# The last product of a decoder block by one level of Strassen, with sums and LayerNorm in PSUM

## The chip, the cores and the metric

The kernel runs on one core of a Trainium2 chip. A core has five engines with a queue of instructions each: TensorE (PE), VectorE (DVE), ScalarE (ACT), GpSimd (POOL) and SyncE (SP), which here only issues DMAs. They meet through semaphores. Matmuls write to PSUM, which PE, DVE and ACT use here; everything else lies in SBUF (128 partitions) or in DRAM. The metric is the device time of one execution in microseconds; "us" below always means that.

## The reference

One block of a decoder: x is 2048 x 1024 in float32. A projection feeds two branches, a dilated attention and a gated linear recurrence; each is projected to 1024 columns and the two are merged by gates. Only the end concerns this change:

```
merged = sigmoid(gA) * yA + sigmoid(gB) * yB
out    = merged @ W_out + b_out          # (2048 x 1024) @ (1024 x 1024)
x      = LayerNorm(alpha * x + out)      # alpha = 2 ** 0.25, eps = 1e-5, gain and bias by column
```

Here yA = o @ w_attn_proj, with 512 columns of attention output o. `y_a` in the text is this product, `z` is merged @ W_out.

## The kernel before

Products in float32 are made of pieces: each operand is split into a high part h (a rounded copy by ACT) and a low part l (the rest, one subtraction on DVE), and a product is h·h + h·l + l·h, three matmuls for each 128 of the inner dimension. A matmul has a stationary tile of 128 x 128 and moves 512 columns as a rule.

The program has four stages. **Stage A** is the input projection, 507 products of 12 matmuls (line 634), already by one level of Strassen; beside it a planner starts chains of work (ropes, gates, the recurrence, blocks of weights). A chain is a generator that yields an `Ask`: it goes on once a given number of products has passed, enough buffers are vacant, and each engine it names still has budget at this product (`left`). The helper `tt` (line 227) records most of DVE's operations, so they show up under its line. **Attention** comes second (lines 1038 to 1103), the 32 jobs of y_b third (lines 1370 to 1376). The **last stage** has:

- `ya_job(i)` (lines 1440 to 1454), 32 jobs (four chunks of 512 rows, eight blocks of 128 columns): 12 matmuls; DVE multiplies by the gate, reading PSUM (line 1453); POOL adds y_b and writes the merged piece `me` (line 1454). The loads of the gate `gA` and of `ybr` stand on SP.
- `out_job(tt)` (lines 1469 to 1525), 16 row tiles of 128 rows: 48 matmuls into two PSUM banks (lines 1480 to 1482), with `mh`, `ml` of the tile as stationary side and W_out as moving one. `split_m` makes them for the next tile (ACT line 1466, DVE line 1467). Then DVE makes alpha·x + b_out (line 1489), adds both banks (1493), takes statistics (1496, 1499); ACT the root (1513); DVE three small refinements (1515 to 1519), and centre, gain and bias (1503, 1523); ACT's queue issues the stores.
- The first 8 `ya_job`s run alone; the other 24 stand between the row tiles, two to four after a tile, so that their loads and their DVE and POOL work spread over z.
- W_out is split by `split` (lines 1132, 1133) piece by piece, in the eight first `ya_job`s and before.

The order in this stage is that of the code: it is written out by hand, and each engine runs its own queue in it. `later(n, fn)` puts work off by n jobs; `big(slot, ...)` gives one of the large SBUF buffers, X0 to X5 and Z0 to Z2, whose earlier tenant must be done.

Of the kernel before, what the change touches and what calls it, by code (L numbers as in the profile page):

```python
# [31 lines left out]
def hybrid_block_kernel(ctx: ExitStack, tc: tile.TileContext, a: dict, out: bass.AP):  # L32
# [1319 lines left out]
    cmb = {4 + (3 * i) // 2: divmod(i, 4) for i in range(16)}
    wo = [(k, j) for k in range(4) for j in range(2)] + [(4, 0), (5, 0), (4, 1), (5, 1), (6, 0), (7, 0), (6, 1), (7, 1)]
# [37 lines left out]
    for n in range(32):  # L1391
        c, f = divmod(n, 8)
        if c + 1 < NCH:
            for k in range(2 * f, 2 * f + 2) if f < 4 else ():
                load_h(c + 1, k, min(k + 2, 7) - f)
        elif f < 4:
            for k in range(2 * f, 2 * f + 2):
                prep_wa(k, k + 2 - f if k < 6 else 4)
        if n in (12, 14, 28, 29, 30, 31):
            load_wo({12: 0, 14: 1, 28: 2, 29: 3, 30: 4, 31: 5}[n])  # L1400
# [37 lines left out]
    ME, XR, MS = {}, {}, {}  # L1438

    def ya_job(i):  # L1440
        c, f = divmod(i, 8)
        if i + 3 < 8 or 11 <= i + 3 < 32:
            load_ya(i + 3)
        ga, yb = YG.pop(i)
        ya = fp.tile([P, CH], F32, tag="y", name=f"ya{c}{f}", bufs=4)
# [5 lines left out]
        if f == 0:  # L1451
            ME[c] = big(("Z0", "Z1")[c % 2], [P, 8, CH], F32, f"me{c}")
        dve.scalar_tensor_tensor(out=ga, in0=ga, scalar=1.0, in1=ya, op0=ALU.add, op1=ALU.mult)
        pool.tensor_tensor(out=ME[c][:, f], in0=ga, in1=yb, op=ALU.add)
# [5 lines left out]
    def split_m(tt, ks=slice(0, 8)):  # L1460
        c, b = divmod(tt, 4)
        m = ME[c][:, ks, b * P:(b + 1) * P]
        if ks.start == 0:
            MS[tt] = tuple(vx_p.tile([P, 8, P], F32R, tag=t, name=f"{t}{tt}", bufs=2) for t in ("mh", "ml"))
        mh, ml = (t[:, ks] for t in MS[tt])
        act.activation(mh, m, AF.Copy)
        dve.tensor_tensor(out=ml, in0=m, in1=flat(mh), op=ALU.subtract)

    def out_job(tt):
        rows = slice(tt * P, (tt + 1) * P)  # L1470
        x = XR.pop(tt)
        mh, ml = MS.pop(tt)
        last = tt == 15
        parts = [slice(0, CH), slice(CH, CH + 256), slice(CH + 256, D)] if last else [slice(0, CH), slice(CH, D)]
        zz = [fp.tile([P, CH], F32, tag="z", name=f"z{tt}{n}", bufs=3)[:, 0:hs.stop - hs.start] for n, hs in enumerate(parts)]
        for k0, k1 in ((0, 6), (6, 8)) if tt == 0 else ((0, 8),) if tt % 4 else ((0, 7), (7, 8)):
            for z, hs in zip(zz, parts):
                for k in range(k0, k1):
                    w = WO[k]
                    pe.matmul(z, mh[:, k], w[:, 0, hs], start=(k == 0), stop=False)  # L1480
                    pe.matmul(z, mh[:, k], w[:, 1, hs], start=False, stop=False)  # L1481
                    pe.matmul(z, ml[:, k], w[:, 0, hs], start=False, stop=(k == 7))  # L1482
        if tt + 1 < 16:
            load_xr(tt + 1)
            split_m(tt + 1, slice(0, 8 if (tt + 1) % 4 else 7))
        if tt == 1:
            for fn in at1:
                fn()
        dve.scalar_tensor_tensor(out=x, in0=x, scalar=ALPHA, in1=vec[0], op0=ALU.mult, op1=ALU.add)
        st_ = cst.tile([P, 4, 6], F32, tag="st", name=f"st{tt}", bufs=2)  # L1490
        n = 0
        for z, hs in zip(zz, parts):
            dve.tensor_tensor(out=x[:, hs], in0=x[:, hs], in1=z, op=ALU.add)
            step = 256 if last else CH
            for q in range(hs.start, hs.stop, step):
                dve.bn_stats(out=st_[:, n, :], in_=x[:, q:q + step])
                n += 1
        mv = cst.tile([P, 4], F32, tag="mv", name=f"mv{tt}", bufs=2)
        dve.bn_aggr(out=mv[:, 0:2], in_=st_[:, 0:n])
        halves = (slice(0, CH), slice(CH, D))  # L1500

        def centre(hs):
            dve.scalar_tensor_tensor(out=x[:, hs], in0=x[:, hs], scalar=mv[:, 0:1], in1=vec[1][:, hs],
                                     op0=ALU.subtract, op1=ALU.mult)

        if last:
            pool.memset(mv[:, 3:4], -0.5)
            pool.tensor_tensor(out=mv[:, 2:3], in0=mv[:, 1:2], in1=epst, op=ALU.add)
            pool.tensor_tensor(out=mv[:, 2:3], in0=mv[:, 2:3], in1=mv[:, 3:4], op=ALU.pow)
            for hs in halves:  # L1510
                centre(hs)
        else:
            act.activation(mv[:, 2:3], mv[:, 1:2], AF.Sqrt, bias=epst)
            centre(halves[0])
            dve.reciprocal(out=mv[:, 2:3], in_=mv[:, 2:3])

            dve.tensor_scalar(out=mv[:, 1:2], in0=mv[:, 1:2], scalar1=EPS, scalar2=-0.5, op0=ALU.add, op1=ALU.mult)
            dve.scalar_tensor_tensor(out=mv[:, 3:4], in0=mv[:, 2:3], scalar=mv[:, 2:3], in1=mv[:, 1:2], op0=ALU.mult, op1=ALU.mult)
            dve.tensor_scalar(out=mv[:, 2:3], in0=mv[:, 3:4], scalar1=1.5, scalar2=mv[:, 2:3], op0=ALU.add, op1=ALU.mult)
        for hs, eng in zip(halves, (sp, act) if last else (act, act)):  # L1520
            if hs.start and not last:
                centre(hs)
            dve.scalar_tensor_tensor(out=x[:, hs], in0=x[:, hs], scalar=mv[:, 2:3], in1=vec[2][:, hs],
                                     op0=ALU.mult, op1=ALU.add)
            eng.dma_start(out[rows, hs], x[:, hs])
# [12 lines left out]

    def bring_at(c):
        if c < NCH:  # L1540
            for k in range(4):
                load_at(c, k, 1)

    load_xr(0)
    load_vec(0)
    bring_at(1)
    load_vec(1)
    load_vec(2)
    for i in range(8, 11):
        load_ya(i)  # L1550
    now["n"] += 1
    for tt in range(16):
        c, b = divmod(tt, 4)
        run(late)
        out_job(tt)
        if c + 1 < NCH:
            for f in (((0, 1), (2, 3), (4, 5, 6), (7,)) if c else ((), (0, 1, 2), (3, 4, 5, 6), (7,)))[b]:
# [64 lines left out]
```

## Time and profile before

| what | value |
|---|---|
| median of three runs | 2084.6 us (2084.38 to 2085.69) |
| the profiled execution: its time | 2088.65 us |
| its span, first to last instruction | 2086.9 us |
| granted clock of PE, mean | 0.998 |
| first matmul of y_a | 1817.98 us |
| first matmul of z | 1839.74 us |

The profiled execution is the one that all durations come from. In the profile a group is a line, an engine, an operation, out<-in and its shape, with count, busy time and mean in ns; a row of the timeline has its start and its duration, and in brackets the idle time of the engine before it and what ended that. A window row has, for each engine, the busy time and the number of instructions (x), then PE's granted clock, the share of the DMA engines and GB/s. In the chain of waits PE's rows show the time to the next matmul, not the length of one.

### The profile page before, as it was taken

The numbers are of one execution on the slowest core, as the hardware profiler recorded it, in microseconds if no ns is written. First come the engines' busy times: TensorE is split into PE (matmuls) and PEld (weight loads), VectorE is DVE, ScalarE is ACT, GpSimd is POOL, SyncE is SP. The second block draws the span as 40 slices with busy tenths as digits, with TensorE's granted clock in tenths as the row PEclk, the third lists the DMA queues.
The fourth block names the chain that finished last, engine by engine and source line by source line (L and its number), as shares of the span: only waits on it lengthen the run. The fifth ranks groups of instructions, "written<-read, shape, count | busy, mean of one in ns | idle before, by whom it ended". The sixth has DMA issues, their size and how long they took to land.

```text
span 2086.9 us, 35149 instructions
## 1 busy us (share of the span) xinstructions
PE 2066.7 (99%) x11696; PEld 1704.5 (82%) x11696; DVE 1657.9 (79%) x3146; ACT 1101.7 (53%) x2293; POOL 471.6 (23%) x436
## 2 busy tenths in 40 slices
PE   8999999999999999999999999999999999999998
PEld 7888887887878888888887888888888888888887
DVE  8888889788888878778878888877999545576667
ACT  6447356346356565667666657567999411211100
POOL 1111111111111012222222232221425244331120
PEclk9999999999999999999999999999999999999999
DMA  9997988988988977778788979789896898964432
GB/s 277 276 255 240 265 256 240 289 253 264 249 282 236 323 251 195 233 209 242 235 258 261 287 233 266 246 227 365 323 334 196 246 300 276 300 226 159 145 106 71
DMA packets 370358, 516.27 MB, mean 247 GB/s; under 512 B 173824, under 2 KB 178944, under 8 KB 366848
## 3 DMA queue, kind: packets, MB, share of 16 engines
q1 hardware_dynamic: 350000, 480.63, 72.5%
q0 software_dynamic: 12256, 19.42, 5.5%
q10 hardware_dynamic: 7920, 13.97, 1.8%
q8 instruction: 93, 1.52, 0.3%
q14 instruction: 89, 0.73, 0.1%
HBM read 312.95 MB, written 186.25 MB: 239 GB/s over the span
## 4 chain that ended last, share of the span: by engine, by line
PE 66%; ACT 5%; DVE 1%; DMA 0%; issue 0%; DVEq 0%; ACTq 0%
PE q L634 39%; ACT p L1053 4%; PE yb L1370 3%; PE yb L1371 3%; PE z L1480 3%; PE z L1482 3%; PE yb L1372 3%; PE z L1481 3%; PE o L1094 2%; PE s L1038 2%; PE ya L1448 1%; PE ya L1450 1%; PE ya L1449 1%; PE pt L1064 1%; PE g L495 1%; PE bc L1312 1%
## 5 line engine op out<-in xcount | busy, mean ns | idle before, releaser
L634 PE MATMUL q<-xT,hS 128*128 128x512 f32 x1680 | 519.0, 390 | 0.2 <-DVE v L227 0.2
L634 PE MATMUL q<-xT,l 128*128 128x512 f32 x1120 | 435.8, 389 | 0.0
L634 PE MATMUL q<-xB,hA 128*128 128x512 f32 x1248 | 388.6, 393 | 5.6 <-ACT xB L215 5.5
L634 PEld LDWEIGHTS q<-xT,hS 128*128 128x128 f32 x1680 | 314.2, 188 | 70.4 <-issue 5.8
L634 PE MATMUL q<-xB,l 128*128 128x512 f32 x904 | 353.1, 391 | 1.1 <-DVE l L227 1.1
L634 PEld LDWEIGHTS q<-xB,hA 128*128 128x128 f32 x1248 | 235.2, 189 | 58.5 <-ACT xB L215 5.5
L634 PEld LDWEIGHTS q<-xT,l 128*128 128x128 f32 x1120 | 210.2, 188 | 44.0 <-DVE l L227 0.2
L634 PEld LDWEIGHTS q<-xB,l 128*128 128x128 f32 x904 | 170.5, 189 | 37.4 <-DVE l L227 1.9
L1053 ACT ACTIVATE p<-p,sta 128x256 f32<-128x256 f32 (+1 forms) x384 | 172.7, 469 | 1.1 <-DVE sta L1045 1.1
L634 PE MATMUL q<-xT,hA 128*128 128x512 f32 x560 | 173.0, 390 | 0.0
L634 PE MATMUL q<-xB,hS 128*128 128x512 f32 x560 | 172.9, 390 | 0.0
L245 POOL DMA_DIRECT2D wS<-in_w_in_dram x70 | 61.8, 967 | 485.6 <-DMA wS<-in_w_in_dram 174.6
L269 ACT ACTIVATE hA<-wA 128x512 fp32r<-128x512 f32 x218 | 134.2, 623 | 49.8 <-DMA wA<-in_w_in_dram 13.3
L269 ACT ACTIVATE hS<-S 128x512 fp32r<-128x512 f32 x175 | 107.8, 623 | 82.9 <-DVE S L227 17.6
L227 POOL TENSOR_TENSOR S<-S,wA 128x512 f32<-128x512 f32 x35 | 50.0, 1428 | 351.7 <-DVE S L227 266.8
L634 PEld LDWEIGHTS q<-xT,hA 128*128 128x128 f32 x560 | 104.7, 188 | 23.4 <-issue 1.8
L634 PEld LDWEIGHTS q<-xB,hS 128*128 128x128 f32 x560 | 104.8, 188 | 23.1 <-issue 1.5
L1045 DVE CUSTOM_DVE_ANT_0 p<-s,mask 128x256 f32<-128x256 f32 (+1 forms) x384 | 116.5, 360 | 0.2 <-PE s L1038 0.2
L1481 PE MATMUL z<-wo,mh 128*128 128x512 f32 (+1 forms) x264 | 101.0, 383 | 0.0
L1482 PE MATMUL z<-wo,ml 128*128 128x512 f32 (+1 forms) x264 | 101.0, 383 | 0.0
L1480 PE MATMUL z<-wo,mh 128*128 128x512 f32 (+1 forms) x264 | 101.0, 383 | 0.0
L1370 PE MATMUL yb<-h,wl 128*128 128x512 f32 x256 | 100.3, 392 | 0.0
(204 smaller groups left out, 4134.9 us busy)
## 6 DMA issues: line engine op xcount, KB each, us to landing
wA<-in_w_in_dram SPq DMA_DIRECT2D x253, 256.0 KB, 4.7
wl_scr<-l SPq DMA_DIRECT2D x105, 512.0 KB, 5.0
l<-wl_scr SPq DMA_DIRECT2D x105, 512.0 KB, 4.4
sw<-y SPq DMA_DIRECT2D x384, 64.0 KB, 3.2
wS<-in_w_in_dram SPq DMA_DIRECT2D x70, 256.0 KB, 4.6
wS<-in_w_in_dram POOLq DMA_DIRECT2D x70, 256.0 KB, 6.7
v_scr<-vs SPq DMA_DIRECT2D x192, 64.0 KB, 3.6
B<-k_scr SPq DMA_DIRECT2D x24, 512.0 KB, 7.6
```

Of the source, the lines that this page charges most:

```text
L227: eng.tensor_tensor(out=out, in0=in0, in1=in1, op=op)
L245: pool.dma_start(t, w_part(s, x), accum_op=ALU.add)
L269: act.activation(h, r, AF.Copy)
L634: pe.matmul(bank, w[:, ks], x[:, kk, xx], start=(first and i == 0 and not onto), stop=(last and i == 11), skip_group_check=onto)
L1045: dve.tensor_tensor_reduce(out=st["p", i, j][:, h, lo:256], in0=st["s", i, j // 2][h][:, j % 2, lo:256], in1=mask[:, lo:256], scale=1.0, s ...
L1053: act.activation(p, p, AF.Exp, scale=-1.0, bias=s[:, h:h + 1], accum_out=s[:, 2 + h:3 + h])
L1370: pe.matmul(yb, WL[f][:, 0, k], xx[:, 0], start=(k == 0), stop=False)
L1371: pe.matmul(yb, WL[f][:, 0, k], xx[:, 1], start=False, stop=False)
L1372: pe.matmul(yb, WL[f][:, 1, k], xx[:, 0], start=False, stop=(k == 7))
L1480: pe.matmul(z, mh[:, k], w[:, 0, hs], start=(k == 0), stop=False)
L1481: pe.matmul(z, mh[:, k], w[:, 1, hs], start=False, stop=False)
L1482: pe.matmul(z, ml[:, k], w[:, 0, hs], start=False, stop=(k == 7))
```

## The change

1. **Blocks of W_out in stage A.** `out_blocks(kk)`, four chains that start at products 26, 78, 98 and 132, load four tiles of W_out, make Strassen's differences T1 = B12 - B11, T3 = B22 - B12, T2 = B22 - T1, T4 = B21 - T2 on DVE, split each into h and l, and store them to DRAM (`wt_scr`). Only B11, B21 and B22 are still split late: 12 splits for 16.
2. **y_a whole first.** All 32 `ya_job`s run before z. Merged pieces of chunks 0 and 1 stay in SBUF; those of chunks 2 and 3 are left in the gate's buffer and stored (`m_scr`), and `load_me` brings a chunk back later, 2 MB each.
3. **z by Strassen.** A quad is 256 rows; it has seven products of 12 matmuls of 512 columns instead of two tiles of 48. POOL makes the sums S1 to S4 of merged pieces (`add_m`), ACT and DVE split each unit (`prep_m`, three buffers each).
4. **Sums in PSUM.** ACT seeds a bank with b_out (`seed`), the products add to it, and `z_outs` makes alpha·x plus a bank in another bank on DVE, to which later products add. Four banks per quad: A, C, Z0, Z1. The old PSUM pool `fp` is closed before z.
5. **LayerNorm from PSUM.** Sums and squares are accumulated on ACT, the scale and the shift are one ACT operation in the bank, the gain is DVE's and the bias POOL's; SP issues the stores.
6. **T loads.** T1 to T4 (8 MB) are loaded after y_a, into X2, X3, X1 and X4.

The diff, cut to its core:

```diff
+    def out_blocks(kk):
+        yield Ask(lag=0, need=4, keep=2)
+        r = {}
+        for i in range(2):
+            for j in range(2):
+                t = r[i, j] = take(f"wo{kk}{i}{j}")
+                k = 4 * i + kk
+                sp.dma_start(flat(t), a["w_out"][k * P:(k + 1) * P, j * CH:(j + 1) * CH])
...
+            yield Ask(lag=3 if n == "T1" else 1, DVE=.72)
+            tt(dve, flat(r[z]), flat(r[x]), in1, ALU.subtract)
...
+            yield Ask(need=1, keep=2, ACT=.66, DVE=.72)
+            h, l = take(f"oh{kk}{n}"), raw[n]
+            act.activation(h, flat(l), AF.Copy)
+            tt(dve, l, flat(l), flat(h), ALU.subtract)
+            yield Ask()
+            for x, t in enumerate((h, l)):
+                sp.dma_start(wt_scr[n][:, kk, x], flat(t))
...
+    for kk in K4:
+        at((26, 78, 98, 132)[kk], lambda kk=kk: start_chain(out_blocks(kk), 6))
...
-        pool.tensor_tensor(out=ME[c][:, f], in0=ga, in1=yb, op=ALU.add)
+        pool.tensor_tensor(out=ME[c][:, f] if c < 2 else ga, in0=ga, in1=yb, op=ALU.add)
+        if c > 1:
+            later(1, lambda: sp.dma_start(m_scr[c][:, f], ga))
...
+    def add_m(q, n):
...
+        pool.tensor_tensor(out=t, in0=piece(q, x), in1=piece(q, y), op=op)
+    def prep_m(q, n):
+        h, l = UN[q, n] = [vx_p.tile([P, 4, P], F32R, tag=t, name=f"{t}{q}{n}", bufs=3) for t in ("mh", "ml")]
+        act.activation(h, piece(q, n), AF.Copy)
+        dve.tensor_tensor(out=l, in0=piece(q, n), in1=flat(h), op=ALU.subtract)
+    NQZ = 8
+    order = [(0, 1), (1, 1), (0, 2), (1, 2), (0, 5), (1, 5), (0, 3), (1, 3), (0, 6), (1, 6), (0, 7), (1, 7), (2, 5), (0, 4), (1, 4)]
+    for q in range(2, NQZ):
+        order += [(q, 1), (q, 3), (q, 6)]
+        order += [(q, 2), (q, 7), (q + 1, 5), (q, 4)] if q < NQZ - 2 else [(q, 2), (q, 7), (q + 1, 5)] if q == NQZ - 2 else \
+            [(q - 1, 4), (q, 7), (q, 2), (q, 4)]
...
+    for n in ("T1", "T2", "T3", "T4"):
+        load_tb(n)
...
+    HB = {1: "A", 6: "A", 7: "A", 5: "C", 3: "C", 2: "Z0", 4: "Z1"}
+    def seed(q, n):
+        act.activation(bank(q, n), vec[0][:, lo if n == "A" else hi], AF.Copy)
+    def z_product(g):
...
+                pe.matmul(b, x[:, k], w[:, k, y], start=False, stop=(k == 3 and n == 2), skip_group_check=True)
+    def z_outs(g):
...
+        if p == 1:
+            scaled(bank(q, "Z0"), x0[:, lo], of(q, "A"))
+        elif p == 5:
+            scaled(x1[:, hi], x1[:, hi], of(q, "C"))
+        elif p == 3:
+            scaled(x0[:, hi], x0[:, hi], of(q, "C"))
+        elif p == 6:
+            tt(dve, of(q, "C"), x0[:, hi], of(q, "A"), ALU.add)
+        elif p == 7:
+            scaled(bank(q, "Z1"), x1[:, lo], of(q, "A"))
+            tt(dve, of(q, "A"), x1[:, hi], of(q, "A"), ALU.add)
...
+        act.activation(of(q, n), of(q, n), AF.Copy, accum_out=s[:, j:j + 1])
...
+            act.activation(y[j], of(q, n), AF.Square, bias=s[:, 2:3], accum_out=s[:, 3 + j:4 + j])
...
+        act.activation(s[:, 6:7], s[:, 5:6], AF.Sqrt, scale=1.0 / D, bias=epst)
...
+            act.activation(of(q, n), of(q, n), AF.Identity, scale=s[:, 10:11], bias=s[:, 11:12])
...
+            tt(dve, y[j], of(q, n), vec[1][:, hs], ALU.mult)
...
+            tt(eng, y[j], y[j], vec[2][:, (lo, hi)[j]], ALU.add)
...
+    LN = (("Z0", "C"), ("Z1", "A"))
...
+            g = max(ready) + 1
+            on(g, "square", lambda q=q, i=i: ln_square(q, i))
+            on(g + 1, "root", lambda q=q, i=i: ln_root(q, i))
+            on(g + 1, "scale", lambda q=q, i=i: ln_scale(q, i))
+            on(g + 2, "gain", lambda q=q, i=i: ln_gain(q, i))
+            on(g + 3, "store", lambda q=q, i=i: ln_store(q, i))
+        if place[q, 1] >= 2:
+            on(place[q, 1] - 1, "seed", lambda q=q: seed(q, "A"))
+        on(place[q, 5] - 1, "seed", lambda q=q: seed(q, "C"))
...
+    for g in range(NZ + 6):
+        if g < NZ:
+            z_product(g)
+        for k in ("seed", "load", "add", "gain", "root"):
+            do(g, k)
+        if g + 2 < NZ:
+            q, p = order[g + 2]
+            prep_m(q, UNIT[p])
+        for k in ("scale", "sum", "square"):
+            do(g, k)
+        if g < NZ:
+            z_outs(g)
+        do(g, "store")
```

Product p of a quad, in the text (q,p): 1 is A11·B11 and 2 is A12·B21, 3 is S4·B22 and 4 is A22·T4, 5 is S1·T1, 6 is S2·T2, 7 is S3·T3, where A11 to A22 are the quarters of the quad's merged rows.

How the queues stand in the middle of z. First ACT before the change, around row tiles 5 and 6 (`mh` is the copy for the next tile, `mv` the root, DMA a store):

```order
L1466 ACTIVATE mh6_21249<-me1_20782 128x1024 [waits PE_49,Activation_49]
L1513 ACTIVATE mv5_21259<-mv5_21259,epst_20415 128x1 [waits DVE_49]
L1525 DMA out_0_dram<-x5_21133 128x512 [waits DMAHW4_49,DVE_49]
L1525 DMA out_0_dram<-x5_21133 128x512 [waits DMAHW5_49,DVE_49]
L1466 ACTIVATE mh7_21362<-me1_20782 128x1024 [waits PE_49,Activation_49]
L1513 ACTIVATE mv6_21372<-mv6_21372,epst_20415 128x1 [waits DVE_49]
L1525 DMA out_0_dram<-x6_21247 128x512 [waits DMAHW3_49,DVE_49]
L1525 DMA out_0_dram<-x6_21247 128x512 [waits DMAHW4_49,DVE_49]
```

ACT after, in quad 2 (`y20` are the squares of its row tile 0, `mv20` that tile's smalls, `Z02`, `C2`, `A2`, `A3` banks of PSUM, `mh3A11` the copy for the first product of quad 3):

```order
L1628 ACTIVATE y200_21747,mv20_21719<-Z02_21646,mv20_21719 128x512 [waits DMAHW3_49,DVE_49,Pool_49]
L1628 ACTIVATE y201_21748,mv20_21719<-C2_21508,mv20_21719 128x512 [waits DMAHW4_49,Pool_49]
L1633 ACTIVATE mv20_21719<-mv20_21719,epst_20544 128x1 [waits DVE_49]
L1518 ACTIVATE mh3A11_21772<-me1_20748 128x512 [waits PE_49]
L1643 ACTIVATE Z02_21646<-Z02_21646,mv20_21719 128x512 [waits DVE_49]
L1643 ACTIVATE C2_21508<-C2_21508,mv20_21719 128x512
L1621 ACTIVATE A2_21601,mv21_21783<-A2_21601 128x512
L1583 ACTIVATE A3_21798<-vec0_20594 128x512
L1518 ACTIVATE mh3S4_21804<-smS43_21739 128x512 [waits PE_49,Pool_49]
L1518 ACTIVATE mh3S2_21822<-smS23_21737 128x512 [waits PE_49]
```

Four instructions per row tile, two of them stores, have become about twelve of 512 columns; the seed of bank A3, to which the first product of quad 3 adds, stands behind the root, the two scalings and the sum of quad 2.

DVE before, in row tile 5 (`ml` is the low part for tile 6, `z50` the first bank, `st5`, `mv5` statistics):

```order
L1467 TENSOR_TENSOR ml6_21250<-me1_20782,mh6_21249 128x1024 [waits Activation_49]
L1489 SCALAR_TENSOR_TENSOR x5_21133<-x5_21133,vec0_20584 128x1024 [waits DMAHW2_49,DMAHW1_49]
L1493 TENSOR_TENSOR x5_21133<-x5_21133,z50_21197 128x512 [waits DVE_49,PE_49]
L1496 BN_STATS st5_21254<-x5_21133 128x6 [waits DVE_49]
L1493 TENSOR_TENSOR x5_21133<-x5_21133,z51_21198 128x512 [waits PE_49]
L1496 BN_STATS st5_21254<-x5_21133 128x6 [waits DVE_49]
L1499 BN_AGGR mv5_21259<-st5_21254 128x2 [waits DVE_49]
L1503 SCALAR_TENSOR_TENSOR x5_21133<-x5_21133,mv5_21259,vec1_20591 128x512 [waits DVE_49]
L1515 RECIPROCAL mv5_21259<-mv5_21259 128x1 [waits Activation_49]
L1517 TENSOR_SCALAR mv5_21259<-mv5_21259 128x1
```

DVE after, at the end of product (2,7) (line 1597 combines x with a bank, line 229 is the helper `tt`, line 1519 the low part, lines 1637 to 1640 the smalls):

```order
L1597 SCALAR_TENSOR_TENSOR Z12_21751<-x5_21512,A2_21601 128x512 [waits PE_49]
L229 TENSOR_TENSOR A2_21601<-x5_21512,A2_21601 128x512
L229 TENSOR_TENSOR mv20_21719<-mv20_21719 128x1 [waits Activation_49]
L1519 TENSOR_TENSOR ml3A11_21773<-me1_20748,mh3A11_21772 128x512 [waits DVE_49,Activation_49]
L1637 TENSOR_SCALAR mv20_21719<-mv20_21719 128x1 [waits DVE_49]
L1638 RECIPROCAL mv20_21719<-mv20_21719 128x1
L1639 SCALAR_TENSOR_TENSOR mv20_21719<-mv20_21719 128x1 [waits DVE_49]
L1640 TENSOR_SCALAR mv20_21719<-mv20_21719 128x1 [waits DVE_49]
L229 TENSOR_TENSOR mv20_21719<-mv20_21719 128x1 [waits DVE_49]
L1597 SCALAR_TENSOR_TENSOR x7_21550<-x7_21550,C3_21735 128x512 [waits DMAHW5_49,PE_49]
L229 TENSOR_TENSOR y200_21747<-Z02_21646,vec1_20640 128x512 [waits DMAHW3_49,Activation_49,Pool_49]
L229 TENSOR_TENSOR y201_21748<-C2_21508,vec1_20640 128x512 [waits DMAHW4_49,Activation_49,Pool_49]
```

The row tile's additions of z and its statistics are gone from DVE. The sum of squares (`mv20`) and the smalls now stand behind both combinations after product 7, with one low part between them.

SP before, at the last y_a pieces (loads of the gate, of y_b and of x):

```order
L1387 DMA ybr30_21760<-yb_scr_74 128x512 [waits DMAHW6_49,Pool_49]
L1458 DMA x11_21828<-in_x_dram 128x1024 [waits DMAHW7_49,DMAHW5_49]
L1386 DMA gA31_21853<-mg_scr_73 128x512 [waits DMAHW0_49,DVE_49]
L1387 DMA ybr31_21854<-yb_scr_74 128x512 [waits DMAHW1_49,Pool_49]
L1458 DMA x12_21952<-in_x_dram 128x1024 [waits DMAHW5_49,DMAHW4_49,DMAHW2_49]
L1458 DMA x13_22044<-in_x_dram 128x1024 [waits DMAHW4_49,DMAHW3_49,DVE_49]
L1458 DMA x14_22119<-in_x_dram 128x1024 [waits DMAHW6_49,DMAHW7_49,DMAHW0_49,DVE_49]
L1458 DMA x15_22194<-in_x_dram 128x1024 [waits DMAHW2_49,DMAHW1_49,DVE_49]
```

SP after, at the same pieces (`m_scr3` is the DRAM copy of chunk 3's merged rows, `toT1` a T block):

```order
L1481 DMA m_scr3_182<-gA28_21094 128x512 [waits DMAHW6_49,Pool_49]
L1481 DMA m_scr3_182<-gA29_21114 128x512 [waits DMAHW7_49,Pool_49]
L1481 DMA m_scr3_182<-gA30_21134 128x512 [waits Pool_49]
L1481 DMA m_scr3_182<-gA31_21154 128x512 [waits DMAHW1_49,Pool_49]
L1492 DMA toT1_21222<-wt_scrT1_177 128x1024 [waits DMAHW2_49,PE_49,Activation_49]
L1492 DMA toT1_21222<-wt_scrT1_177 128x1024 [waits DMAHW3_49]
L1492 DMA toT1_21222<-wt_scrT1_177 128x1024 [waits DMAHW4_49]
L1492 DMA toT1_21222<-wt_scrT1_177 128x1024 [waits DMAHW5_49]
L1492 DMA toT2_21227<-wt_scrT2_178 128x1024 [waits DMAHW6_49,PE_49]
L1492 DMA toT2_21227<-wt_scrT2_178 128x1024 [waits DMAHW7_49]
```

The loads of T blocks stand behind the last stores of merged pieces, which wait for POOL; the loads of x behind the T blocks.

More of the change, by code (lines that the diff above doesn't have):

```diff
@@ L1398, in hybrid_block_kernel @@
                 prep_wa(k, k + 2 - f if k < 6 else 4)
[L1399 to L1400 removed]
+        for _ in range(2 if n in (12, 14, 28, 29, 30, 31) else 0):
+            load_wo(*wo_raw.pop(0))
         if n == 26:
@@ L1460, in split_m @@
[L1460 to L1525, printed above, removed]
```

212 lines of the change are left out of this document (155 added, 57 removed).

## The prediction

> **What bounds the kernel now.** First the page: its engine line and the times.
>
> ```profile
> span 2086.9 us, 35149 instructions
> PE 2066.7 (99%) x11696; PEld 1704.5 (82%) x11696; DVE 1657.9 (79%) x3146; ACT 1101.7 (53%) x2293; POOL 471.6 (23%) x436
> ```
>
> TensorE is busy for 99% of the span. That is a mean over stages, so next I read the busy time in stretches of the last stage, where most of the change lies.
>
> ```profile
> core 0: us, PE busy (x) PEld busy (x) DVE busy (x) ACT busy (x) POOL busy (x), PEclk, DMA share, GB/s
> 1840.00:1860.00 20.00, 20.00 (x90) 16.57 (x89) 12.71 (x21) 6.09 (x9) 1.67 (x1) 1.00 0.87 302
> 1920.00:1940.00 20.00, 20.00 (x90) 16.57 (x89) 15.83 (x25) 2.42 (x3) 5.11 (x4) 1.00 0.39 132
> 2040.00:2060.00 20.00, 20.00 (x90) 16.57 (x89) 14.58 (x24) 2.91 (x5) 0.35 (x1) 1.00 0.24 80
> 2060.00:2080.00 20.00, 19.57 (x109) 16.99 (x108) 15.66 (x30) 1.36 (x2) 0.10 (x1) 1.00 0.14 54
> 2080.00:2087.00 7.00, 0.00 (x0) 0.00 (x0) 3.49 (x7) 0.00 (x0) 1.08 (x2) 0.72 0.20 75
> ```
>
> PE is busy 20.00 of 20 us at a granted clock of 1.00 until the last product; DVE is at 12 to 16 of 20, ACT below 7. So PE bounds this stage, every removed matmul is time, and what is added beside it is free only while PE finds its operands. The last row is the tail: no PE for 7 us. Next, the cadence and the end of the chain of waits.
>
> ```profile
> 1830.68 0.39 PE L1450 MATMUL ya<-at,wa 128*128 128x512 f32 x1
> ...
> 1839.74 0.39 PE L1480 MATMUL z<-wo,mh 128*128 128x512 f32 x1
> ...
> 1843.37 0.39 PE L1481 MATMUL z<-wo,mh 128*128 128x512 f32 x1
> 2077.42 0.12 PE z L1480
> 2077.54 0.12 PE z L1481
> 2079.46 0.13 PE z L1482
> 2079.61 0.43 DVE x L1493
> ...
> 2082.93 0.66 DVEq L1618
> L1480 PE MATMUL z<-wo,mh 128*128 128x512 f32 x248 | 96.5, 389 | 0.0
> L1448 PE MATMUL ya<-at,wa 128*128 128x512 f32 x128 | 49.8, 389 | 0.0
> ```
>
> Between the first and third row lie 56 starts: 12.69 / 56 = 0.2266 us per 512-column matmul (its 0.39 us is pipelined). A product of 12 is 2.72 us. The halves of the last tile go at 0.12.
>
> **Terms of the sum**, against the profiled execution (2088.65 us, span 2086.9; the median shown is 2084.6, 4.05 less, and I carry that offset).
>
> *Removed from PE.* z now is 3 x 248 = 744 matmuls of 512 columns and 3 x 16 = 48 of 256: 744 x 0.2266 + 48 x 0.12 = 174.4 us. After, it is 8 quads x 7 products x 12 = 672 matmuls: 152.3. **-22.1 us.** The 384 matmuls of y_a stay; only their order changes.
>
> *Tail.* Now the span ends 2086.9 - 2079.59 = 7.3 us after the last matmul, 3.97 of it behind DVE's last start at 2082.93. Rows for the new tail, which reads sums and squares on ACT:
>
> ```profile
> L658 ACT ACTIVATE e<-q x70: 572/598/638, 35.7 to 1409.7; 128x512 f32<-128x512 f32 x70
> L1053 ACT ACTIVATION_READ_ACCUMULATOR p<-p,sta x384: 185/203/271, 1430.9 to 1626.9; 128x1 f32 x192
> L469 ACT ACTIVATE v<-ub,lr,lrn x32: 816/817/820, 89.8 to 1343.6; 128x512 f32<-128x512 f32 x32
> L1513 ACT ACTIVATE mv<-mv,epst 128x1 f32<-128x1 f32 x15 | 4.4, 295 | 124.8 <-DVE mv L1499 124.8
> L1513 ACT ACT_TABLE_LOAD x1 | 1.3, 1283 | 0.0
> L1493 DVE TENSOR_TENSOR x<-x,z 128x512 f32<-128x512 f32 x31 | 21.2, 685 | 37.2 <-PE z L1482 36.0
> 1853.19 0.16 DVE L1515 RECIPROCAL mv<-mv 128x1 f32<-128x1 f32 x1
> 1853.94 0.75 DVE L1523 SCALAR_TENSOR_TENSOR x<-x,mv,vec 128x512 f32<-128x512 f32 x1
> L1315 POOL TENSOR_TENSOR oc<-oc x32: 1288/1292/1301, 1673.5 to 1806.9; 128x512 f32<-128x512 f32 x32
> ```
>
> A PSUM row costs ACT 0.60, with a sum read out 0.20 more; a scale and bias 0.82; the small DVE chain 0.75 for four and so about 1.0 for five; a POOL add 1.29. Row tile 14 is ready one product (2.72) before the end, and its sum 0.8, small 0.2, squares 1.6, small 0.2, root 0.3, smalls 1.0, two scalings 1.6 stand ahead of tile 15 on ACT: 5.7, so 3.0 of it lies behind the last matmul. Tile 15 then pays sum 0.8, small 0.2, squares 1.6, small 0.2, root 0.3, smalls 1.0, one scaling 0.82, gain 0.69, two POOL adds 2.6, some 0.4 of hand-overs: 8.6. With 3.97 for the stores 15.6 stands against 7.3. **+8.3** (6 to 10).
>
> *A quad in the middle.* Per quad PE has 7 x 2.72 = 19.04 us, and the seed of the next quad's A bank is a row of ACT's queue behind this chain: product 7 ends; DVE makes two combinations from PSUM (starts 0.60 apart: 1.2); the small sum of squares (0.21); ACT's root (0.30) and copy of the next mh (0.53); DVE's ml (0.60) and five smalls (1.0); ACT's two scalings (1.5), a sum (0.7), the seed (0.59), hand-overs. That is 6.6 us. PE meanwhile has two products, (q+1,5) and (q,4): 5.44. So PE waits 1.2 per quad before anything else goes wrong. Quads 2 to 5 have this order; in quad 6 the seed stands ahead of the root. What may go wrong shows today at a few places, where VectorE and GpSimd meet:
>
> ```profile
> 1832.61 1.67 POOL L1454 TENSOR_TENSOR me<-gA,ybr 128x512 f32<-128x512 f32 x1 [1.11 <-DVE gA L1453]
> 1837.99 1.67 POOL L1454 TENSOR_TENSOR me<-gA,ybr 128x512 f32<-128x512 f32 x1 [0.81 <-DVE gA L1453]
> 1832.45 0.68 DVE L1133 TENSOR_TENSOR wo<-wo 128x512 fp32r<-128x512 f32 x1
> 1833.05 1.78 DVE L1467 TENSOR_TENSOR ml<-me,mh 128x512 fp32r<-128x512 f32 x1
> 1838.43 1.51 DVE L1467 TENSOR_TENSOR ml<-me,mh 128x256 fp32r<-128x256 f32 x1
> 1842.86 0.42 DVE L1467 TENSOR_TENSOR ml<-me,mh 128x256 fp32r<-128x256 f32 x1 [1.63 <-ACT mh L1466]
> ```
>
> The same 256-column ml takes 1.51 us begun inside a POOL add and 0.42 with POOL idle; the 512-column subtract 1.78 against 0.68. Both end when the add does: 1.1 us lost each. Operations with an input in PSUM (L1493, 0.685 on average) show nothing of the kind. Before, POOL is nearly empty here (0.35 to 5.1 of 20 us above); after, it has 8 adds per quad, four sums and four biases, 10.3 to 13.4 us of 19, beside seven ml subtracts and small operations with two SBUF inputs. [...] In the chain I charge one blocked ml (1.1) and, since POOL is in an add more than half the time, half of another for the two-input smalls (0.5): 1.2 + 1.6 = 2.8 a quad. Below, the chain alone is 1.2, or nothing if it is shorter than I count; above, every two-input small blocked: 5.2. **4 x 2.8 = +11.2** (0 to 21).
>
> *Start of z.* ml of the first product stands on DVE behind the last y_a combination, which waits for y_a's last matmul: 0.39 + 0.69 + 0.60 against the two matmuls (0.45) that need only mh. **+1.05** (1 to 3).
>
> *Product (2,5).* Its seed stands on ACT behind the first root's table load (1.28), a copy, a sum and squares that wait for the first quad's smalls. **+3** (0 to 3.6). Last quads, whose order is tighter: **+2** (0 to 4).
>
> *T blocks at z.* 16 loads of 512 KB are issued only behind the last store of merged pieces; T1 is needed four products (10.9 us) after z starts. At the 302 GB/s of the 1840 stretch 2.1 MB take 7 us. **+0.5** (0 to 4).
>
> *T blocks in stage A.* 32 DVE and 16 ACT operations, 16 loads and 32 stores of 256 KB. At a DVE cadence of 0.60 that is 19 us on DVE and 9 on ACT, spread over products 26 to about 165, and none on PE.
>
> ```profile
> 60.00:160.00 100.00, 100.00 (x444) 82.29 (x443) 84.80 (x152) 45.20 (x80) 14.33 (x19) 1.00 0.91 261
> 319.52 0.50 PE L634 MATMUL q<-xB,l 128*128 128x512 f32 x1 [1.07 <-DVE l L227]
> 320.87 0.50 PE L495 MATMUL g<-vh,gw 64*128 64x512 f32 x2 [0.15 <-ACT vh L485]
> 321.68 0.77 PE L495 MATMUL g<-vl,gw 64*128 64x512 f32 x2 [0.31 <-DVE vl L227]
> 322.00:324.00 2.00, 2.00 (x7) 1.16 (x6) 2.00 (x4) 0.85 (x2) 0.85 (x2) 0.50 0.90 297
> 324.00:326.00 2.00, 2.00 (x8) 1.58 (x7) 2.00 (x5) 0.79 (x2) 0.89 (x2) 0.71 0.86 196
> ```
>
> DVE has 15 us of slack in 100 there and DMA 0.09, so the cover is thin: at 320 us one late subtract already cost PE 1.07, 0.15 and 0.31 us. **+1** (-2, if the shift removes that gap, to +5).
>
> The sum: -22.1 + 8.3 + 11.2 + 1.05 + 3 + 2 + 0.5 + 1 = **+5.0**; 2088.65 + 5.0 - 4.05 = **2089.6 us**.
>
> **Rivals.**
> (B) *The seed chain without blocked subtracts.* POOL's adds may fall between the chains, since they wait for ACT and DVE too. Then a quad costs 1.2: 11.2 becomes 4.8, the sum -1.4: 2083.2. For it: only a few operations are blocked now; against: POOL's share more than doubles.
> (C) *PE stays dense*, the faster side: hand-overs hide in two products of buffering, the quads and (2,5) cost nothing, and what is left is -22.1 + 8.3 + 1.05 + about 1: 2072.9. It decides from a chain shorter than 5.44 us, 1.2 below my count. For it: DVE and ACT each have some 13 of 19 us to do; against: the count is from rows.
> (D) *The clock falls in the gaps*, slower. After the 1.07, 0.15 and 0.31 us gaps within 3 us the granted clock was 0.50 and 0.71 for two stretches of 2 us: 1.0 + 0.6 us lost. Case A's gaps of 2.8 us a quad would do this at four to six places, 6 to 10 us: 2096 to 2100. It decides from gaps of about 1.5 us close together. [...] Stage A at its upper end would come to the same size.
> That the change doesn't do what it says I leave out: the 672 matmuls stand in the program.
>
> **How the numbers follow.** A 0.42, B 0.25, C 0.20, D 0.13. 0.2% (4.2 us) is about what a measurement of this kernel can tell from no change: faster is below 2080.4, slower above 2088.8. A is slower in two thirds of its spread (2085 to 2096), else the same; B mostly the same (2079 to 2087); C faster; D slower. Slower 0.28 + 0.13 = 0.41, faster 0.20 + 0.08 = 0.28, the same 0.31. Of both signs, A's own range is 2085 to 2096; 8 in 10 needs C's centre and D's: 2073 to 2100, and the ends of the unknown costs lie mostly within.
>
> **What would show it.** PE idle before the first matmul of products (3,1) to (6,1), ended by ACT's seed, 1.2 us each in B and 2.8 in A; ml groups with a mean near 0.7 (B, C) or above 1.0 (A); a wait at (2,5); 15.6 us behind the last matmul; a granted clock under 1.00 in the z stretches for D; DVE-ended PE waits in the first 500 us for the T blocks. The prediction is wrong if the chain after product 7 is under 5.4 us, or if the T loads or stage A cost several us.

## The result, and the profile after

The changed kernel takes 2148.34 us (2146.54 to 2150.07, 4 runs) against 2085.14: the ratio is 1.0303, 95% interval 1.0285 to 1.0321. It is 63 us slower; the forecast was 2089.6 with a range up to 2100. The side was right, by far not the size. The first lines of the page of the profile after, then its waits of PE, the longest first:

```profile
span 2147.3 us, 35530 instructions
PE 2063.4 (96%) x11576; PEld 1689.9 (79%) x11576; DVE 1665.1 (78%) x3180; ACT 1201.0 (56%) x2517; POOL 562.8 (26%) x497
```

```profile
engine line waited for: us in total, times, longest us
PE q L636 <- DVE l L229: 9.8, 6, 2.3
PE g L497 <- DVE vl L229: 9.2, 6, 4.5
PE A L1590 <- DVE C L229: 8.6, 5, 1.8
PE A L1590 <- ACT A L1583: 8.3, 4, 2.1
PE A L1590 <- DVE ml0A L1519: 6.6, 1, 6.6
PE q L636 <- ACT xB L217: 5.6, 1, 5.6
PE A L1590 <- DVE Z L1597: 4.1, 2, 3.7
PE C L1590 <- ACT C L1583: 3.1, 1, 3.1
```

PE was 99% busy and is now 96%. The first two rows lie in stage A, where the change adds nothing but the four chains of W_out; the rows of line 1590 are z. The stage lengths, in us, from the starts of PE's matmuls:

| stretch | before | after | difference |
|---|---|---|---|
| start to first attention product | 1428.7 | 1457.4 | +28.7 |
| first attention product to the first y_a product (attention and y_b) | 389.3 | 389.4 | +0.1 |
| first y_a product to the last matmul | 261.3 | 282.4 | +21.1 |
| last matmul to the end of the span | 7.6 | 18.1 | +10.5 |

The last two rows are the last stage, 268.9 us before and 300.5 after. The sum is 60.4, the difference of the spans. The 96 removed matmuls are real (1056 x 0.2266 = 239.3 us of work are left in the third row), so 43 us of waiting and of lower clock stand in that row. The timeline of PE shows them (in brackets the idle time and what ended it):

```profile
1941.11 0.80 PE L1590 MATMUL A<-woB,ml0A 128*128 128x512 f32 x1 [6.63 <-DVE ml0A L1519]
1979.18 0.74 PE L1590 MATMUL C<-toT,mh2S 128*128 128x512 f32 x2 [3.06 <-ACT C L1583]
2000.03 0.70 PE L1590 MATMUL A<-toT,mh2S 128*128 128x512 f32 x2 [3.66 <-DVE Z L1597]
2008.70 0.69 PE L1590 MATMUL A<-toT,mh2S 128*128 128x512 f32 x2 [1.37 <-DVE C L229]
2019.24 0.73 PE L1590 MATMUL A<-woB,mh3A 128*128 128x512 f32 x2 [2.09 <-ACT A L1583]
2032.47 0.70 PE L1590 MATMUL A<-toT,mh3S 128*128 128x512 f32 x2 [1.82 <-DVE C L229]
2042.96 0.73 PE L1590 MATMUL A<-woB,mh4A 128*128 128x512 f32 x2 [2.09 <-ACT A L1583]
2056.13 0.70 PE L1590 MATMUL A<-toT,mh4S 128*128 128x512 f32 x2 [1.82 <-DVE C L229]
```

A quad in the middle takes 2042.96 - 2019.24 = 23.72 us for 19.04 of matmuls: 4.68 lost, 2.8 was charged. It has two waits: 2.09 us on the seed, as forecast, and 1.82 us on the bank of product 7. Ahead of the first row y_a's last loads are late: z's first low part stands behind them and PE idles 6.63 us. From there to 2019.24 it loses another 18.8 us: 78.1 us for 262 matmuls, which are 59.4 at 0.2266.

### The profile page after: what moved, and what is told of

It is laid out like the page before. It is cut to its first block, busy times and chain, and to the rows that moved or that the text cites. A ratio compares the mean times of both kernels' runs of the same rounds, so it can differ in the third digit from the quotient of the medians.

```text
span 2147.3 us, 35530 instructions
## 1 busy us (share of the span) xinstructions
PE 2063.4 (96%) x11576; PEld 1689.9 (79%) x11576; DVE 1665.1 (78%) x3180; ACT 1201.0 (56%) x2517; POOL 562.8 (26%) x497
## 4 chain that ended last, share of the span: by engine, by line
PE 57%; DMA 10%; ACT 9%; DVE 8%; issue 7%; SPq 4%; POOL 4%; DVEq 0%; POOLq 0%; ACTq 0%
PE q L636 43%; ACT p L1083 6%; PE yb L1394 3%; PE yb L1395 3%; PE yb L1396 3%; SPq L309 2%; DVE l L229 2%; DMA wA<-in_w_in_dram 2%; POOL smS L1514 2%; DMA wS<-in_w_in_dram 2%; POOL y L229 1%; DMA sw<-y 1%; DVE y L229 1%; DMA m_scr<-gA 1%; PE g L497 1%
## 5 line engine op out<-in xcount | busy, mean ns | idle before, releaser
L271 ACT ACTIVATE hS<-S 128x512 fp32r<-128x512 f32 x175 | 108.1, 624 | 85.5 <-DVE S L229 16.8
L1394 PE MATMUL yb<-h,wl 128*128 128x512 f32 x256 | 100.2, 392 | 0.0
L1395 PE MATMUL yb<-h,wl 128*128 128x512 f32 x256 | 99.9, 390 | 0.0
L1396 PE MATMUL yb<-h,wl 128*128 128x512 f32 x256 | 99.7, 389 | 0.0
L229 DVE TENSOR_TENSOR y<-y,cos 128x512 f32<-128x512 f32 x96 | 81.9, 858 | 22.5 <-DMA sw<-y 18.6
```

What stands on the lines that cost most here:

```text
L229: eng.tensor_tensor(out=out, in0=in0, in1=in1, op=op)
L271: act.activation(h, r, AF.Copy)
L1394: pe.matmul(yb, WL[f][:, 0, k], xx[:, 0], start=(k == 0), stop=False)
L1395: pe.matmul(yb, WL[f][:, 0, k], xx[:, 1], start=False, stop=False)
L1396: pe.matmul(yb, WL[f][:, 1, k], xx[:, 0], start=False, stop=(k == 7))
```

## Experiments

Each run was executed once. They were made in four groups, and the kernel before, executed beside each group on the same chip, took 2086.39 us (sa_full to sa_asks), 2086.51 (sa_asks2 to z_nopool), 2086.74 (z_dve to best1) and 2084.07 (best2, best3). "A" is the time of the first attention product, "last" the stretch from the first y_a product to the end of the span; sa_asks, which ran at another clock, is told below. Five traces with the same stage A, that of the changed kernel and four of its variants, have A from 1455.7 to 1459.8, so 2 us of A either way mean nothing.

| run | us | A | last |
|---|---|---|---|
| before / after (medians) | 2085.14 / 2148.34 | 1428.7 / 1457.4 | 268.9 / 300.5 |
| sa_full | 2114.89 | 1454.3 | 269.4 |
| sa_compute | 2101.50 | 1441.4 | 269.0 |
| sa_dma | 2114.23 | 1454.1 | 268.9 |
| sa_asks2 | 2086.22 | 1426.1 | 268.9 |
| sa_tiny | 2094.89 | 1434.7 | 269.0 |
| sa_late | 2095.07 | 1435.0 | 269.0 |
| z_nopool | 2121.28 | 1456.5 | 273.7 |
| z_dve | 2138.19 | 1459.8 | 287.3 |
| z_order | 2148.40 | 1457.2 | 300.1 |
| ya_stage | 2139.52 | 1455.7 | 292.6 |
| best1 | 2120.55 | 1443.6 | 285.0 |
| best2 | 2112.54 | 1441.7 | 279.8 |
| best3 | 2107.43 | 1438.8 | 277.6 |

**Stage A.** First the four chains alone, put into the kernel before:

> The kernel before plus only the four chains that make T1 to T4 in stage A; nothing reads their stores, the last stage is that of before. If stage A's loss in the changed kernel (its first attention product came at 1457.4 us against 1428.7) belongs to these chains alone: 2113 us median, +28, with the first attention product near 1457. If y_a and z in their new form take part in it: under +15.

+28.5, and the last stage is as before: stage A's loss of 28.7 belongs to them. Then they were taken apart, with the same askings, so that the planner moves the other chains alike. The lines that each run leaves out:

```diff
# sa_compute: no stores
             for x, t in enumerate((h, l)):
-                sp.dma_start(wt_scr[n][:, kk, x], flat(t))
# sa_dma: no work on DVE and ACT; the stores send the raw tile l twice
-            tt(dve, flat(r[z]), flat(r[x]), in1, ALU.subtract)
...
-            act.activation(h, flat(l), AF.Copy)
-            tt(dve, l, flat(l), flat(h), ALU.subtract)
# sa_asks: neither, and no loads
```

> As sa_full, without the 32 stores; the 16 loads, 32 VectorE and 16 ScalarE operations and all their askings stay. Theory DVE (the added VectorE work makes the low parts late): nearly all of the loss stays, +20 to +28. Theory DMA (issues and traffic on SyncE's queue): about a third of it, +5 to +10. Theory PLAN (the askings alone push other chains aside): as sa_asks.

> As sa_full, without the VectorE and ScalarE operations: 16 loads and 32 stores (of the raw tiles) and all askings stay. Theory DVE: within 5 us of the kernel before. Theory DMA: +20 to +28. Theory PLAN: as sa_asks.

> As sa_full, with no instruction left in the chains: only their buffers are taken and their askings spend the planner's budget, so that the other chains move as in the changed kernel. Theories DVE and DMA: within 5 us of the kernel before. Theory PLAN: +20 or more.

The transfers without any VectorE work cost +27.8, as theory DMA has it. The VectorE work with 16 loads and no stores costs +15.1, between the bounds of the two theories. The execution of sa_asks took 2925.29 us at a granted clock of 0.65 and says nothing of the chains. The same kernel was run again, and beside it a run that parts the entries in SyncE's queue from the bytes:

> The kernel of sa_asks once more (its execution had a granted clock of 0.65 from end to end). The 48 transfers with no VectorE work cost +27.8 us, loads and VectorE work without stores +15.1. Theory DMA: with neither, within 5 us of the kernel before. Theory PLAN (the askings displace other chains): +15 or more.

> As sa_dma (48 transfers, no VectorE or ScalarE work), but each transfer takes 8 of the 128 partitions: 16 KB for 256. Theory ISSUE (48 more entries in SyncE's queue, some 0.5 us each and in order): +20 to +28 as in sa_dma. Theory TRAFFIC (12.6 MB on transfer engines that are 0.9 busy): that part goes, near sa_asks2. Theory PLAN: as sa_asks2.

```diff
# sa_tiny: sa_dma with 8 of 128 partitions in each transfer (the loads likewise)
-                sp.dma_start(wt_scr[n][:, kk, x], flat(l))
+                sp.dma_start(wt_scr[n][0:8, kk, x], flat(l)[0:8])
```

-0.3 and +8.4. Displacing other chains costs nothing, 48 more entries in SyncE's queue (with 0.8 MB) 8.4 us, and the bytes the other 19.4 of 27.8: theory PLAN falls, and sa_tiny lies between ISSUE and TRAFFIC, nearer to TRAFFIC. DVE's work on top of all transfers adds 0.7 (28.5 against 27.8). How the 15.1 of sa_compute divide between that work and its 4.2 MB of loads is not shown: no run has the work without loads. The windows of 60 to 450 us, where nearly all of these transfers are issued (the loads of W_out from 83 us, the last store at 460 in sa_dma), first of the kernel before and then of sa_dma:

```profile
60.00:450.00 390.00, 388.47 (x1712) 317.01 (x1711) 330.62 (x538) 200.93 (x328) 56.88 (x71) 1.00 0.90 258
```

```profile
60.00:450.00 390.00, 374.56 (x1629) 303.54 (x1628) 312.11 (x510) 193.51 (x314) 51.73 (x64) 0.98 0.93 273
```

The transfer engines go from 0.90 to 0.93, and less of everything else gets done: 1629 matmuls for 1712, and DVE, which has no more work in sa_dma, is busy for 312 us, not 331. So DVE waits. The waits in the same window tell on what; the kernel before, then sa_dma:

```profile
DVE S L227 <- DMA wS<-in_w_in_dram: 10.8, 6, 2.6
ACT hA L269 <- DMA wA<-in_w_in_dram: 4.1, 3, 1.7
DVE S L227 <- DMA wA<-in_w_in_dram: 2.8, 3, 1.2
```

```profile
ACT hA L270 <- DMA wA<-in_w_in_dram: 14.2, 7, 4.5
DVE S L228 <- DMA wA<-in_w_in_dram: 10.4, 5, 4.5
DVE S L228 <- DMA wS<-in_w_in_dram: 9.9, 6, 3.9
```

In these rows the waits of ACT and DVE for tiles of w_in go from 17.7 to 34.5 us. PE names DVE's low part as what it waited for, which is only the end of that chain. In the changed kernel itself it can be followed: DVE waits for a load of w_in, and the low part `vl` stands behind it in DVE's queue, with five operations between.

```profile
263.87 0.69 DVE L229 TENSOR_TENSOR S<-wS,wA 128x512 f32<-128x512 f32 x1 [3.16 <-DMA wS<-in_w_in_dram]
268.14 0.79 PE L497 MATMUL g<-vl,gw 64*128 64x512 f32 x2 [4.49 <-DVE vl L229]
```

SyncE's own waits in this window differ little between the two runs that part entries from bytes (107.5 us in all in sa_tiny, 105.7 in sa_dma), so its queue is not what sets them apart. How the bytes make these loads late stays open. The sum of such waits does not rank the runs (the same three rows give 26.5 us in sa_tiny and 24.4 in sa_full), and the median time of a load of w_in from issue to landing hardly moves: 4.9, 6.7 and 4.3 us for its three kinds before, 4.9, 7.2 and 4.5 in sa_dma.

> As sa_full, with the chains started at products 258, 300, 350 and 400 and only when twelve buffers are vacant, behind the first 600 us where the kernel before has its few late operands. If the loss belongs to the place (DMA share 0.90 and a late low part now and then in the first 600 us, 0.75 to 0.86 and none after): below +5 us. If the same work costs the same anywhere in stage A: +20 or more.

```diff
-        at((26, 78, 98, 132)[kk], lambda kk=kk: start_chain(out_blocks(kk), 6))
+        at((258, 300, 350, 400)[kk], lambda kk=kk: start_chain(out_blocks(kk), 6))
-        yield Ask(lag=0, need=4, keep=2)
+        yield Ask(lag=0, need=4, keep=8)
```

+8.6: above the 5 that I asked for, far below 20. The place, together with the demand for more vacant buffers, decides most of it. What is left stands in the first row of PE's waits, again a transfer that is late, but another one: PE itself waits for a load of pieces from DRAM.

```profile
PE q L635 <- DMA l<-wl_scr: 9.3, 3, 5.9
```

**z.**

> The changed kernel without GpSimd's work in z: the sums S1 to S4 are replaced by raw pieces and the bias of the LayerNorm is left out. Theory BLOCK (two-input VectorE operations wait for POOL's adds): the wait before product 7 of a quad (1.82 now) goes and the one on the seed (2.09) falls to about 1.0; a quad takes 20.0 to 20.5 us for 23.7; 2148 falls by 18 to 22. Rival CHAIN (the order of the queues alone): a quad stays above 22.5 us, the total falls by less than 6.

(The sums are raw pieces and the LayerNorm's bias is missing in this run.) The last stage falls by 26.8 us and the total by 27.1, more than the 18 to 22 that were expected. A quad takes 2070.51 - 2050.16 = 20.35 us; the wait before product 7 is gone and the one on the seed is what the chain alone was forecast to cost (0.97 idle plus the slower start):

```profile
2050.16 0.74 PE L1589 MATMUL A<-woB,mh5A 128*128 128x512 f32 x2 [0.96 <-ACT A L1582]
2070.51 0.73 PE L1589 MATMUL A<-woB,mh6A 128*128 128x512 f32 x2 [0.97 <-ACT A L1582]
```

How the price was paid stands in two groups, first of the changed kernel, then of z_nopool: the small operation ahead of the squares (128 x 1, two inputs in SBUF) and the low parts of sums.

```profile
L1625 DVE SCALAR_TENSOR_TENSOR mv<-mv,sum_t 128x1 f32<-128x1 f32 x16 | 13.7, 858 | 7.0 <-ACT Z L1621 4.7 <-ACT C L1621 2.3
L1519 DVE TENSOR_TENSOR ml3S<-smS,mh3S 128x512 fp32r<-128x512 f32 x4 | 5.8, 1460 | 0.9 <-ACT mh3S L1518 0.9
```

```profile
L1624 DVE SCALAR_TENSOR_TENSOR mv<-mv,sum_t 128x1 f32<-128x1 f32 x16 | 3.5, 217 | 7.0 <-ACT Z L1620 4.7 <-ACT C L1620 2.3
L1518 DVE TENSOR_TENSOR ml3S<-me,mh3S 128x512 fp32r<-128x512 f32 x4 | 2.7, 686 | 1.0 <-ACT mh3S L1517 1.0
```

0.858 against 0.217 us, 1.460 against 0.686. The first mean is a mixture: ten of the sixteen took 1.24 us and six 0.22. Each of the ten ends 0.01 to 0.02 us after an add of POOL; of the six, five stand where POOL is idle and one (2129.49) inside a pair of its adds. So an operation on one column lost 1.02 us in ten of sixteen rows, about as much as the one on 512 columns in the forecast's rows (1.78 against 0.69 us), and that is what I had undercounted. (The two subtracts of the forecast's rows end 0.55 and 0.28 us after their adds, not with them; low parts of 512 columns in z of the changed kernel lose up to 1.1.) The timeline of the changed kernel, POOL's row first, shows a collision:

```profile
2020.75 3.44 POOL L1514 TENSOR_TENSOR smS<-me 128x512 f32<-128x512 f32 x2
2019.76 3.28 DVE L1519 TENSOR_TENSOR ml3S<-smS,mh3S 128x512 fp32r<-128x512 f32 x2 [0.90 <-ACT mh3S L1518]
2022.97 1.24 DVE L1625 SCALAR_TENSOR_TENSOR mv<-mv,sum_t 128x1 f32<-128x1 f32 x1
2024.13 0.68 DVE L1597 SCALAR_TENSOR_TENSOR Z<-x,A 128x512 f32<-128x512 f32 x1
```

DVE's three operations ahead of the last row take 4.52 us here and 1.59 in z_nopool (2 x 0.686 + 0.217), POOL's two adds 3.44 for 2 x 1.29 (POOL at 1952.94: 1.29). The combination from PSUM in the last row takes 0.68 us, no longer than in z_nopool (0.70), and so does one that runs wholly inside POOL's adds (at 2031.64: 0.68); the one here is late only because it stands behind.

> The changed kernel with the sums S1 to S4 and the bias of the LayerNorm on VectorE instead of GpSimd; nothing is left out. Theory BLOCK: no GpSimd instruction runs beside z's two-input operations, VectorE gets eight operations of 0.60 more per quad (about 18 of 19 us), a quad takes 20.3 to 21.5 us for 23.7 and the total falls by 14 to 25. Rival LOAD (VectorE was the bottleneck of z by its work, not by waiting): a quad takes 23.7 or more and the total does not fall.

```diff
-        pool.tensor_tensor(out=t, in0=piece(q, x), in1=piece(q, y), op=op)
+        dve.tensor_tensor(out=t, in0=piece(q, x), in1=piece(q, y), op=op)
-    def ln_gain(q, i, eng=pool):
+    def ln_gain(q, i, eng=dve):
```

A quad takes 2062.37 - 2041.40 = 20.97 us and DVE is busy 16.8 of 20. The last stage falls by 13.2; the total by 10, as stage A came out 2.4 later. BLOCK holds for the quads in the middle, on a kernel that leaves nothing out. The total misses the 14 that were expected: the first quads lose as much as before (78.1 us from 1942.35 to 2020.47, too), though no GpSimd instruction runs beside them.

> The changed kernel with two places of the order moved: the seed of the next quad's A bank one product earlier, ahead of the root, scalings and sum, and product (2,5) behind (0,4) and (1,4). Theory CHAIN (the seed's place in ScalarE's queue): the waits on the seed (2.09 at four places) and the 3.06 at (2,5) go, the total falls by 8 to 13. Rival: what is late behind VectorE comes late anyway, the wait moves to product 7 and the total falls by less than 5.

```diff
-        [..., (0, 7), (1, 7), (2, 5), (0, 4), (1, 4)]
+        [..., (0, 7), (1, 7), (0, 4), (1, 4), (2, 5)]
-            on(place[q, 1] - 1, "seed", lambda q=q: seed(q, "A"))
+            on(place[q, 1] - 2, "seed", lambda q=q: seed(q, "A"))
```

Nothing gained: the rival's time. The waits on the seed are gone, but (2,3) now waits 7.95 us, and a quad in the middle still takes 22.60 (2079.21 - 2056.61). VectorE is late: the wait before product 7 stays at 1.78, and one of 0.99 before product 6 takes the place of that on the seed.

```profile
2001.27 1.19 PE L1590 MATMUL C<-woB,mh2S 128*128 128x512 f32 x2 [7.95 <-DVE x L1597]
2056.61 0.70 PE L1590 MATMUL A<-toT,mh4S 128*128 128x512 f32 x2 [1.78 <-DVE C L229]
2071.71 0.70 PE L1590 MATMUL A<-toT,mh5S 128*128 128x512 f32 x2 [0.99 <-DVE Z L1597]
2079.21 0.70 PE L1590 MATMUL A<-toT,mh5S 128*128 128x512 f32 x2 [1.78 <-DVE C L229]
```

**The start of z.** In the changed kernel the last y_a combination waits for its gate, whose load waits for a store out of the same buffer. The chain of waits there (cut where the dots are):

```profile
1927.79 6.56 DMA m_scr<-gA
1934.37 5.27 DMA gA<-mg_scr
...
1939.77 0.69 DVE gA L1478
1940.45 0.61 DVE ml0A L1519
...
1941.11 7.82 PE A L1590 x22
```

> The changed kernel with the merged pieces of chunks 2 and 3 put into the six buffers of mh and ml, which are idle in y_a, and stored from there, so that a gate's buffer is free after GpSimd's add instead of after the store. Theory HOLD (gate loads wait for stores): the 6.63 us wait at z's first low part falls to 1 to 2 and the stretch of half clock behind it goes, total -5 to -9. Rival TRAFFIC (the transfer engines are 0.9 busy in y_a and the loads are late by that): the wait stays above 4.

```diff
-        pool.tensor_tensor(out=ME[c][:, f] if c < 2 else ga, in0=ga, in1=yb, op=ALU.add)
+        m = ME[c][:, f] if c < 2 else vx_p.tile([P, CH], F32, tag=("mh", "ml")[f % 2], name=f"ms{c}{f}", bufs=3)
+        pool.tensor_tensor(out=m, in0=ga, in1=yb, op=ALU.add)
```

The wait falls to 0.48 us (with 0.22 ahead of it on a seed), the last stage by 7.9, the total by 8.8. HOLD.

**Together.**

> All of it: late T blocks as in sa_late, sums and bias on VectorE, both moves of order, staged stores. If the causes add up: 2148 - 20 - 20 - 9 - 7 = 2092, between 2083 and 2102. Above 2105 the causes overlap.

2120.55, 28.5 above the 2092 of the sum, but not by an overlap alone: two terms of that sum were wrong. The work on VectorE had given 10, not 20, and the moves of order nothing, not 9; here, too, the move of (2,5) brings a wait of 7.33 us before (2,3). And stage A ends at 1443.6, not at the 1435.0 of sa_late; why is not known. So two more, without the moves:

> The changed kernel with late T blocks, sums and bias on VectorE, and staged stores; the order of z's products as in the changed kernel. If the three causes add up by their runs (-20, -10, -9): 2109, between 2105 and 2114.

> As best2, with the first fifteen products of z in another order: quad 1 follows quad 0 by about four products instead of one. Theory BANKS (two LayerNorms at once hold all eight banks and ScalarE's queue): 5 to 12 us below best2. Rival: the loads of the T blocks, now needed earlier, or VectorE's work bound this stretch; within 3 us of best2 or above it.

```diff
# best3 over best2
-    order = [(0, 1), (1, 1), (0, 2), (1, 2), (0, 5), (1, 5), (0, 3), (1, 3), (0, 6), (1, 6), (0, 7), (1, 7), (2, 5), (0, 4), (1, 4)]
+    order = [(0, 1), (1, 1), (0, 2), (1, 2), (0, 5), (0, 3), (0, 6), (0, 7), (1, 5), (0, 4), (1, 3), (1, 6), (1, 7), (2, 5), (1, 4)]
```

best2 came to 2112.54, within its bounds: in the last stage -13.2 and -7.9 give 279.4, measured 279.8. best3 is 5.1 lower, of which 2.2 lie in the last stage and the rest in a stage A that is the same program in both; BANKS explains little. None of them reaches the kernel before. In best3 the stretch from the first y_a product to the last matmul is 261.2 us, as before the change (261.3): waits still eat all that the removed matmuls gave.

## Why the prediction was wrong, step by step

- *Removed from PE*, -22.1: right. 1056 matmuls stand in the last stage, at the old cadence wherever nothing is late.
- *T blocks in stage A*, +1 (-2 to 5): **this step failed**, it measures +28.7. I named the 0.09 of slack of the transfers and called the cover thin, but priced only VectorE and one late subtract, and never set the bytes against that slack. The row I quoted (share 0.91 at 261 GB/s) would have told: 12.6 MB at 261 / 0.91 = 287 GB/s are 44 us of all engines, and 0.09 of the 390 us are 35. That division says that there is no room, not what it costs. The transfers alone cost 27.8 (sa_dma), most of it by their bytes (sa_tiny).
- *A quad in the middle*, 2.8: the mechanism was right on both parts, the size not. The chain alone is 1.3 (z_nopool: 20.35 against 19.04), as worked out; GpSimd's work beside it costs 3.4 instead of 1.6, since ten of the sixteen small operations ahead of the squares take 1.24 us for 0.22 and the delays meet again before product 7. Of the 3.4, 2.75 go when the same work stands on VectorE (z_dve). The 0.5 a quad for small operations, and with it the bound of 5.2 with every small operation blocked, was an estimate that no row of the kernel before shows: its small operation with two inputs (L1518) takes 0.22 us in all 15 rows. Still the bound was the better value; the measured 4.68 lies next to it.
- *Start of z*, +1.05 (1 to 3): the order on DVE was right, but I took y_a's last load as being in time. It measures 6.63 of idle time plus a lower clock behind; the cause is the store out of the gate's buffer (ya_stage: 0.48 without it), a wait that the change adds and that I did not follow. **This step failed too.**
- *Product (2,5)*, +3: the row says 3.06. But the whole stretch up to the first product of quad 3 loses 18.8, where I had about 6 (this and one quad). z_nopool still loses 11.4 there, so some 7 hang on GpSimd's sums and biases, but not on blocking alone: with that work on VectorE (z_dve) the stretch loses 18.8 again. Another order of the products gave back some 2 (best3). What bounds the rest is open.
- *Last quads*, +2 (0 to 4): right. From the first product of quad 6 (2090.31) to the last matmul's start are 38.9 us for 156 matmuls, which take 35.1: 3.8 lost.
- *Tail*, +8.3 (6 to 10): 10.5, a size just above its bounds; z_nopool, without POOL's two adds and its meetings, ends 13.8 us after the start of its last matmul at 2105.80 instead of 18.1, so POOL's share of it is 4.3.
- *T blocks at z*, +0.5: no wait of PE is ended by them.
- *Rivals.* B fell (POOL's adds do meet DVE's operations). C fell. D was half right: the clock was lower after the long waits (0.70 behind 3.06 us), not after those of a quad (1.00 behind 2.09 us).

The side, slower, was right, and it holds for the last stage by itself (+31.6). But nearly half of the +63 comes from stage A, which the forecast put at +1, and 6.8 from the start of z: in good part the side came out right for other reasons than the forecast's, and that part is luck.

## What to carry to other kernels

Work that is put beside a dense PE has to fit the slack of every resource of that stage, the transfers too: set the bytes against the free share x time. Here, with transfer engines 0.9 busy, there was no room for 12.6 MB in 390 us (+27.8 us in sa_dma). Where GpSimd's adds stand beside VectorE's operations with two inputs in SBUF, as here, count how many instructions can meet, small ones too, not how many bytes they handle: a meeting here cost up to 1.1 us, on one column (1.24 us for 0.22) as on 512 (1.78 for 0.69). And when a store is added to a buffer that a load refills, ask when that store is done: here it set the load's time (the store took 6.56 us; in ya_stage, without it, the wait of 6.63 us fell to 0.48).

## What the runs showed of the hardware that was not expected

The granted clock after waits, in windows of the changed kernel: over the 4 us behind the wait of 3.06 us it was 0.70, behind 3.66 us 0.63, behind 2.09 us 1.00. Behind the 6.63 us ahead of z it was 0.66 over 8 us.

```profile
1941.00:1949.00 8.00, 7.89 (x24) 6.29 (x25) 5.01 (x7) 0.86 (x2) 7.92 (x6) 0.66 0.77 246
1979.00:1983.00 4.00, 3.82 (x12) 3.02 (x13) 3.08 (x6) 0.95 (x3) 3.97 (x3) 0.70 0.39 131
2000.00:2004.00 4.00, 3.97 (x12) 3.16 (x13) 3.08 (x7) 1.62 (x6) 2.52 (x2) 0.63 0.19 73
2019.00:2023.00 4.00, 3.76 (x16) 3.11 (x17) 3.24 (x3) 1.85 (x5) 4.00 (x4) 1.00 0.35 131
```

So of the single waits here those of 3 us and more cost another 1 to 3 us (the missing share times the window), those of 2 us nothing (1.00 behind 2.09 us); the shortest of them with a lower clock behind it was 3.06 us. And one execution of sa_asks ran at 0.65 throughout, 2925 us for a program that took 2086 when it was run again; PE's only notable wait in it was the 5.7 us at the start. Its cause is not known.
